# Down projection of a hybrid DiT block: three plain input tiles and twenty pairs, five pairs at a time, in place of seven plain tiles and eighteen pairs, six at a time

## The chip, the cores and the metric

The kernel runs on one core of a Trainium2 chip. The metric is the device time of one execution in microseconds (us). The kernel before was timed in three runs, and its profile is of one more execution.

## The reference

One block of a diffusion backbone over 512 latent tokens of width 2048, with 256 context tokens: a modulated norm, a combined input projection, latent attention beside a short convolution, an output projection, and a gated MLP with a depthwise convolution. All in float32. The change is in the MLP, after its up projection (5504 hidden features, 43 tiles of 128):

```python
def conv_ffn(h, w_up, cw, cb, w_down):
    u = dwconv3(h @ w_up, cw, cb)
    a, g = jnp.split(u, 2, axis=-1)
    return (a * jax.nn.silu(g)) @ w_down
...
x = x + gt_f * conv_ffn(hf_l, w_up[l], ffn_conv_w[l], ffn_conv_b[l], w_down[l])
return rms_norm(x, g_final)
```

`gt_f` is the last of six parts of a modulation vector, silu(c) times `w_ada`.

## The kernel before

Tokens lie along the free dimension (512 columns), features along the 128 partitions. A float32 operand is split into a high and a low part; a product is three matmuls (`mm3`, lines 187 to 189: high x high, high x low, low x high). ACT casts the high part of a weight, DVE subtracts it to get the low one (`split4`, lines 1023 and 1024, with three buffers each).

**Up projection** (to about 1670 us of the profile). Each hidden tile f is made by seven block products, convolved and activated (`acts`). Its result y goes one of two ways, as background work that `pump` feeds in, a piece at a time, after products. The first `STD` = 7 tiles are *plain*: `plain` (line 1050 on) writes high and low part of y to `y_d`. The other 36 make `PAIRS` = 18 pairs: `pair_sums` builds from two tiles and the two halves of the tokens seven half tiles ("11", "21", "2", "1", "3", "4", "22"), each as high and low part in one tile, and ACT sends it to `t_d`.

**Down projection, plain part.** For two halves h of the output and each plain tile k, one weight tile of 1024 columns (`dw`) is split and multiplied into eight banks of 512 columns (tiles `d`, `yl`). Between these steps the code advances `gate_mods`: 32 slices `aq` of `w_ada` (line 1301 loads, line 1303 multiplies with a vector and sums), which give the second half of the gate; they use the pool `tmp` of five buffers. It also loads the first window of pairs (`win_load`, line 1317) and, at `W0_AT`, the weights of the first block step.

**Down projection, block part.** `STEPS` = 24 steps: eight pairs of output tiles, in three rounds of six pairs of input tiles. A step does seven products of `WIN` pairs (`seven`), each of 18 matmuls of 256 columns, named p1, p2, p6, q5, p7, q4, q3 after the block scheme; q4 and q3 of a step run in the next. The names `v12p6h` and `v12p6l` are the high and low part of the weights of p6 of step 12. `into` (line 1389 for the first eight steps, 1392 later) adds a product in PSUM into the output tile `c`. `weights_of` loads four blocks of weights a step ahead and builds sums:

```python
SP.dma_start(z.a11, src[0])
SP.dma_start(z.s1, src[2])
SP.dma_start(z.a12, src[1])
V.tensor_tensor(out=z.s3, in0=z.a11, in1=z.s1, op=ALU.add)
G_.dma_start(z.s1, src[3], accum_op=ALU.add)
```

The accumulating DMA on POOL's queue (line 1345) overwrites s1, so it follows the sum s3 (line 1344); `d_p2` then adds s1 to a11 (line 1405) and a11 to a12 (line 1406) on DVE, and p6, q5 and later products use the results. `gate` (line 1456) multiplies an output tile by the gate and adds the residual `xl`, 16 times in all. Which window of pairs a step uses is given by `SLIDE`: it moves by one pair five times in a round, so that a half tile is seldom loaded twice. All half tiles of the window, the 16 outputs and the y tiles share the pool `t2` of 58 buffers; the weights share nine buffers `raw`.

**The end.** The last two steps are interleaved by hand (`za`, `zb`), with squares, the final norm (`rms_steps`), the scaling of outputs on ACT (`scale_out`, line 1470) and `final`.

The order on each engine isn't the order of the code: a scheduler simulates the program while it is built and puts each instruction where it finds it ready. An engine then runs its list in order.

Of the kernel before, what the change touches and what calls it, by code (L numbers as in the profile page):

```python
# [37 lines left out]
OUT_EARLY = 4  # L38
CTX_EARLY = 6

STD = 7
PAIRS = (NF - STD) // 2
WIN = 6

SLIDE = [0, 0, 1, 2, 3, 4, 5, 5]
STEPS = 8 * PAIRS // WIN

W0_AT = (1, 3)

AHEAD = 3  # L50

# [1 line left out]
def window(st):  # L53

    lo = SLIDE[st % 8] + st // 8 * WIN
    return [(lo + j) % PAIRS for j in range(WIN)]

# [15 lines left out]
def block_kernel(ctx, tc, xt, ctxt, ctxn, c, c_ctx, w_ada, small, w_in, w_inc, w_q, w_kv, w_out,  # L73
# [17 lines left out]
    x_d = dr.tile([NK, P, T], F32, name="x_d")  # L91
    y_d = dr.tile([STD, 2, P, T], F32, name="y_d")
    t_d = dr.tile([PAIRS, 7, P, T], F32, name="t_d")
# [45 lines left out]
    nth = {"raw": 0, "w": 0, "up": 0, "tp": 0}  # L139
# [39 lines left out]
    def part(w, i, n=1):  # L179
        return tuple(z[:, i * P:(i + n) * P] for z in w)  # L180
# [21 lines left out]
    def pump(n=1):  # L202
        while n and bg:
            if next(bg[0], bg) is bg:
                bg.popleft()
            else:
                n -= 1
# [735 lines left out]
    def two(z):  # L943
        return z[:, :T // 2], z[:, T // 2:]
# [75 lines left out]
    def split4(src, n, nm):  # L1020
        hi = rw.tile([P, 1024], F32R, tag="wh", bufs=3, name=nm + "h")
        lo = rw.tile([P, 1024], F32R, tag="wl", bufs=3, name=nm + "l")
        last_hi[:] = [A.copy(out=hi[:, :n], in_=src).ins]
        V.tensor_tensor(out=lo[:, :n], in0=src, in1=hi[:, :n].bitcast(F32), op=ALU.subtract)
        return hi, lo
# [9 lines left out]
    def acts(f, g, a):  # L1035
# [4 lines left out]
        V.tensor_tensor(out=ua, in0=ua, in1=ug, op=ALU.mult)  # L1040
        if f < STD:
            bg.append(plain(f, ua))
        elif (f - STD) % 2 == 0:
            even[0] = ua
        else:
            bg.append(pair_sums((f - STD) // 2, even[0], ua))

    even = [None]

    def plain(f, y):  # L1050

        hi, lo = hilo(y, T, f"yh{f}")
        G_.dma_start(y_d[f, 0], hi.bitcast(F32))
        yield
        G_.dma_start(y_d[f, 1], lo.bitcast(F32))
        yield
# [152 lines left out]
    def product(ps, a, n, nm, first):  # L1209

        w = split4(a, 1024, nm)
        for j in range(8):
            x = operand(n, j)
            if n in APART:
                mm2(ps, part(w, j), x, first and j == 0, j == 7, on_top=not first)
            else:
                mm3(ps[:, :256], part(w, j), x if isinstance(x, tuple) else two(x), first and j == 0, j == 7, on_top=not first)

        nth["up"] += 1
        pump(nth["up"] % 2)  # L1220

    def aside(ps, nm):
        r = cp.tile([P, 256], F32, tag="uu", bufs=4, name=nm)
# [14 lines left out]
    fetched = deque()  # L1238
    plain_order = deque((h, k) for h in range(2) for k in range(STD))

# [69 lines left out]
    gm = gate_mods()  # L1310
# [4 lines left out]
    def win_load(n, p):  # L1315
        z = win[n, p] = t2([P, T], F32R, f"w{n}_{p}")
        SP.dma_start(z.bitcast(F32), t_d[p, OPS.index(n)])

    first = [(n, p) for n in OPS for p in window(0)]
# [10 lines left out]
    def weights_of(st):  # L1330
# [4 lines left out]
        z.out, z.new = (None, None) if nxt == z.win else (z.win[0], nxt[-1])  # L1335
        n = WIN * P
        src = [w_dnw[st][:, b * n:(b + 1) * n] for b in range(4)]
# [14 lines left out]
    for h in range(2):  # L1352
        ps = [bank8(f"d{h}{i}") for i in range(8)]
        for k in range(STD):
            plain_fetch()
            if h == 0 and k + 2 < STD:
                y_load(k + 2)
            w = split4(fetched.popleft(), 1024, f"dw{h}{k}")
            for i in range(8):
                mm3(ps[i], part(w, i), y[k], k == 0, k == STD - 1)  # L1360
            pump(1)
            for _ in range(2):
                next(gm, None)
            for _ in range(2 if h == 0 else 3):
                win_load(*first.pop(0))
            if (h, k) == W0_AT:
                nxt = weights_of(0)
        for i in range(8):
            acc2.append(t2([P, T], F32, f"c{8 * h + i}"))
            A.copy(out=acc2[-1], in_=ps[i])  # L1370
    drain()

    def seven(z, ps, a, n, nm, first, pump_at=()):

        nm = f"v{z.st}{nm}"
        w = split4(a, WIN * P, nm)
        for j, p in enumerate(z.win):
            x = win[n, p]
            mm3(ps[:, :256], part(w, j), (x[:, :256], x[:, 256:]), first and j == 0, j == WIN - 1, on_top=not first)
            if j in pump_at:  # L1380
# [93 lines left out]
    for st in range(STEPS - 2):  # L1474
        z = nxt
        nxt = weights_of(st + 1)
        x_load(st + 1)
        gate(st)
        d_p1(z)
        if first:  # L1480
            for _ in range(4):
                win_load(*first.pop(0)) if first else None
        d_p2(z)
        if prev is not None:
            d_q4(prev)
        d_p6(z)
        d_q5(z)
        next(gm, None)
        if first:
            for _ in range(4):  # L1490
                win_load(*first.pop(0)) if first else None
        if prev is not None:
            d_q3(prev)
            ended(prev)
        d_p7(z)
        prev = z
# [151 lines left out]
```

## Time and profile before

| | |
|---|---|
| three runs | 2136.31, 2138.38, 2142.66 us; median 2138.38 |
| span of the profiled execution, first to last instruction | 2135.4 us |
| mean granted TensorE clock | 0.995 |
| PE, DVE, ACT busy share of the span | 98%, 85%, 49% |
| DMA, mean over the span | 241 GB/s |
| down projection: plain part | about 1670 to 1754 us |
| block part and the end | 1754 to 2135 us |

The profile's own execution is known by its span alone. PE is TensorE's matmuls, PEld its weight loads, DVE the vector engine, ACT the scalar engine, POOL and SP the engines that here mostly issue transfers. A busy PE share says that it always had a matmul under way; whether it was held up is read from the distance of the starts. A window row gives a stretch, its length, the busy time of each engine with the count of instructions, the granted clock, the mean busy share of the 16 DMA engines and GB/s. A timeline row gives start, duration, engine, line, operation, tiles (out<-in, without buffer numbers) and in brackets the idle time before it with what ended that.

### The profile page before, as it was taken

The numbers are of one execution on the slowest core, as the hardware profiler recorded it, in microseconds if no ns is written. First come the engines' busy times: TensorE is split into PE (matmuls) and PEld (weight loads), VectorE is DVE, ScalarE is ACT, GpSimd is POOL, SyncE is SP. The second block draws the span as 40 slices with busy tenths as digits, with TensorE's granted clock in tenths as the row PEclk, the third lists the DMA queues.
The fourth block names the chain that finished last, engine by engine and source line by source line (L and its number), as shares of the span: only waits on it lengthen the run. The fifth ranks groups of instructions, "written<-read, shape, count | busy, mean of one in ns | idle before, by whom it ended". The sixth has DMA issues, their size and how long they took to land.

```text
span 2135.4 us, 35321 instructions
## 1 busy us (share of the span) xinstructions
PE 2084.9 (98%) x13268; PEld 1875.9 (88%) x13268; DVE 1824.1 (85%) x3024; ACT 1047.1 (49%) x1715; POOL 117.0 (5%) x144
## 2 busy tenths in 40 slices
PE   7899999999999999999999999999999999999997
PEld 4688788888888888999999999999999889999996
DVE  7998987778896989898999999999999659888877
ACT  5533333555552337565555555555655433333445
POOL 0000000000000100011000000000000000000000
PEclk9999999999999999999999999999999999999998
DMA  9989876334459986577788788888888989878683
GB/s 335 334 281 322 286 269 202 126 117 159 168 181 355 362 287 216 138 219 210 232 236 241 223 231 243 227 234 231 237 229 232 364 300 309 254 230 240 195 260 107
DMA packets 170176, 513.75 MB, mean 241 GB/s; under 512 B 18962, under 2 KB 23314, under 8 KB 164370
## 3 DMA queue, kind: packets, MB, share of 16 engines
q1 hardware_dynamic: 133364, 418.14, 57.7%
q0 software_dynamic: 17408, 59.25, 14.1%
q10 hardware_dynamic: 19232, 34.09, 4.2%
q8 instruction: 104, 1.70, 0.3%
q14 instruction: 68, 0.56, 0.1%
HBM read 464.22 MB, written 46.14 MB: 239 GB/s over the span
## 4 chain that ended last, share of the span: by engine, by line
PE 89%; DVE 5%; DMA 4%; ACT 2%; issue 1%; SPq 0%; DVEq 0%; POOLq 0%; ACTq 0%
PE pp L187 4%; PE pp L189 4%; PE pp L188 4%; PE o L189 1%; PE o L188 1%; PE o L187 1%; PE d L187 1%; PE d L189 1%; PE d L188 1%; DMA ada<-in_w_ada 1%; PE uf L187 1%; PE uf L188 1%; PE uf L189 1%; PE of L187 1%; PE of L188 1%
## 5 line engine op out<-in xcount | busy, mean ns | idle before, releaser
L1151 POOL DMA_DIRECT2D u_s<-in_w_up x80 | 68.5, 856 | 684.1 <-DMA u_s<-in_w_up 364.4
L263 DVE SCALAR_TENSOR_TENSOR ada<-ada,sv 128x1024 f32<-128x1024 f32 x68 | 81.9, 1217 | 14.0 <-DMA ada<-in_w_ada 14.0
L166 ACT CAST w_0h<-rw 128x512 fp32r<-128x512 f32 (+1 forms) x63 | 38.3, 618 | 107.6 <-PE pp L188 62.3
L241 DVE SCALAR_TENSOR_TENSOR ada<-ada,sv 128x1024 f32<-128x1024 f32 x64 | 77.3, 1215 | 4.3 <-DMA ada<-in_w_ada 4.3
L530 DVE SCALAR_TENSOR_TENSOR ada<-ada,svc 128x1024 f32<-128x1024 f32 x64 | 75.9, 1218 | 3.0 <-DMA ada<-in_w_ada 3.0
L167 DVE TENSOR_TENSOR w_0l<-rw,w_0h 128x512 fp32r<-128x512 f32 (+1 forms) x63 | 42.5, 679 | 21.7 <-ACT w_0h L166 21.6
L263 DVE SCALAR_TENSOR_TENSOR ra<-ra,sv 128x1024 f32<-128x1024 f32 x44 | 52.4, 1215 | 1.0 <-DMA ra<-in_w_ada 1.0
L1265 DVE TENSOR_TENSOR u<-u,u_s 128x1024 f32<-128x1024 f32 x40 | 48.7, 1218 | 1.7 <-DMA u_s<-in_w_up 1.7
L1266 DVE TENSOR_TENSOR u<-u,u 128x1024 f32<-128x1024 f32 x40 | 48.6, 1215 | 0.0
L793 POOL TENSOR_TENSOR gr<-gr,half 128x8 f32<-128x8 f32 x4 | 10.1, 2522 | 631.3 <-DVE gr L792 538.9
L764 ACT CAST pth<-t 128x384 fp32r<-128x384 f32 x64 | 28.6, 485 | 26.4 <-PE t L761 26.4
L1075 DVE TENSOR_TENSOR tp<-a,tp 128x256 fp32r<-128x256 f32 x90 | 37.4, 416 | 2.6 <-ACT tp L1074 2.6
L1074 ACT CAST tp<-a 128x256 fp32r<-128x256 f32 x90 | 35.7, 403 | 4.8 <-DMA yl6h<-y_d 3.5
L1038 ACT ACTIVATE g<-g 128x512 f32<-128x512 f32 x43 | 27.3, 634 | 18.3 <-DVE g L1032 18.0
L541 DVE TENSOR_TENSOR acc<-acc,pp 128x512 f32<-128x512 f32 x50 | 33.9, 677 | 2.1 <-PE pp L189 2.1
L765 DVE TENSOR_TENSOR ptl<-t,pth 128x384 fp32r<-128x384 f32 x64 | 33.1, 547 | 2.7 <-ACT pth L764 2.7
L745 DVE TENSOR_REDUCE mn<-s 128x1 f32<-128x768 f32 x32 | 30.3, 951 | 4.6 <-PE s L734 4.6
L1030 ACT ACTIVATE g<-cg,sm 128x512 f32<-128x512 f32 x40 | 32.6, 815 | 0.0
L1030 ACT ACTIVATE a<-ca,sm 128x512 f32<-128x512 f32 x40 | 32.1, 802 | 0.0
L748 ACT ACTIVATE p<-s,mn 128x768 f32<-128x768 f32 x32 | 29.3, 915 | 1.6 <-DVE mn L745 1.3
L1031 DVE SCALAR_TENSOR_TENSOR g<-cg,sm,g 128x511 f32<-128x511 f32 x40 | 29.8, 745 | 0.0
L1031 DVE SCALAR_TENSOR_TENSOR a<-ca,sm,a 128x511 f32<-128x511 f32 x40 | 29.8, 744 | 0.0
(10238 smaller groups left out, 8906.8 us busy)
## 6 DMA issues: line engine op xcount, KB each, us to landing
ada<-in_w_ada SPq DMA_DIRECT2D x196, 512.0 KB, 6.0
u<-in_w_up SPq DMA_DIRECT2D x120, 512.0 KB, 9.0
w<-t_d SPq DMA_DIRECT2D x161, 256.0 KB, 5.3
u_s<-in_w_up SPq DMA_DIRECT2D x80, 512.0 KB, 4.0
u_s<-in_w_up POOLq DMA_DIRECT2D x80, 512.0 KB, 9.7
t_d<-tp ACTq DMA_DIRECT2D x126, 256.0 KB, 6.0
v<-in_w_dnw SPq DMA_DIRECT2D x72, 384.0 KB, 5.1
ra<-in_w_ada SPq DMA_DIRECT2D x22, 1024.0 KB, 4.7
```

The lines of the kernel that those rows point to most:

```text
L167: V.tensor_tensor(out=lo[:, :n], in0=raw[:, a:a + n], in1=hi[:, :n].bitcast(F32), op=ALU.subtract)
L187: PE.matmul(ps, w[0], x[0], start=first, stop=False, skip_group_check=on_top)
L188: PE.matmul(ps, w[0], x[1], start=False, stop=False, skip_group_check=on_top)
L189: PE.matmul(ps, w[1], x[0], start=False, stop=last, skip_group_check=on_top)
L241: V.scalar_tensor_tensor(out=r, in0=r, scalar=1.0, in1=vec[:, i * 1024:(i + 1) * 1024], op0=ALU.mult, op1=ALU.mult, accum_out=col[:, i:i + 1])
L263: keep(V.scalar_tensor_tensor(out=r, in0=r, scalar=1.0, in1=svs[i], op0=ALU.mult, op1=ALU.mult, accum_out=lc[:, t % 4:t % 4 + 1] if i else ...
L530: keep(V.scalar_tensor_tensor(out=raw[q], in0=raw[q], scalar=1.0, in1=svc[:, q * 1024:(q + 1) * 1024], op0=ALU.mult, op1=ALU.mult, accum_o ...
L1030: A.activation(u, src, AF.Identity, bias=s("fb", m), scale=s("fw", 86 + m))
L1031: V.scalar_tensor_tensor(out=u[:, 1:], in0=src[:, :T - 1], scalar=s("fw", m), in1=u[:, 1:], op0=ALU.mult, op1=ALU.add)
L1151: G_.dma_start(r[-1], src[more], accum_op=ALU.add)
L1265: V.tensor_tensor(out=a11, in0=a11, in1=s1, op=ALU.add)
L1266: V.tensor_tensor(out=a12, in0=a12, in1=a11, op=ALU.add)
```

## The change

Four plain tiles become two more pairs, and the block part takes five pairs at a time in four rounds: 32 steps of 7 x 15 matmuls, where 24 steps of 7 x 18 stood. The plain part shrinks from 14 steps to 6. So do the places at which the slices `aq` and the first window are issued in the code; both are taken in larger portions, and up to two slices in each of the first seven block steps. In the up projection `pump` runs after each of the first twelve products, and after every second one from then on. `W0_AT` moves to the second half's second tile.

```diff
-STD = 7
+STD = 3
 PAIRS = (NF - STD) // 2
-WIN = 6
-SLIDE = [0, 0, 1, 2, 3, 4, 5, 5]
+WIN = 5
+SLIDE = [0, 0, 1, 2, 2, 3, 4, 4]
 STEPS = 8 * PAIRS // WIN
-W0_AT = (1, 3)
+W0_AT = (1, 1)
...
         nth["up"] += 1
-        pump(nth["up"] % 2)
+        pump(1 if nth["up"] <= 12 else nth["up"] % 2)
...
             pump(1)
-            for _ in range(2):
+            for _ in range(3):
                 next(gm, None)
-            for _ in range(2 if h == 0 else 3):
-                win_load(*first.pop(0))
+            for _ in range(5 if h == 0 else 6):
+                if first:
+                    win_load(*first.pop(0))
...
         d_p6(z)
         d_q5(z)
-        next(gm, None)
+        if st < 7:
+            for _ in range(2):
+                next(gm, None)
```

Counted in the built programs: loads of window half tiles 161 before, 168 now; loads of block weights (SP) 96 and 128; accumulating loads (POOL) 24 and 32; plain weights 14 and 6. Line numbers behind the plain loop grow by one: `into` is 1390 and 1393, the first weight sum 1406, `gate` 1457, `scale_out` 1471.

**DVE ahead of the first block product.** `v0p1l` is the low part of its weights, `dw` those of the plain part, `ts`, `a` and `tp` belong to the last pair's half tiles. Before:

```order
2267 L1024 TENSOR_TENSOR dw13l<-d_17796,dw13h 128x1024
2268 L1024 TENSOR_TENSOR dw14l<-d_17843,dw14h 128x1024
2269 L1303 SCALAR_TENSOR_TENSOR aq_17722,lcc<-aq_17722,svq_17417 128x512
2270 L1303 SCALAR_TENSOR_TENSOR aq_17763,lcc<-aq_17763,svq_17417 128x512
2271 L1024 TENSOR_TENSOR dw15l<-d_17885,dw15h 128x1024
2272 L1303 SCALAR_TENSOR_TENSOR aq_17766,lcc<-aq_17766,svq_17419 128x512
2273 L1303 SCALAR_TENSOR_TENSOR aq_17832,lcc<-aq_17832,svq_17419 128x512
2274 L1303 SCALAR_TENSOR_TENSOR aq_17835,lcc<-aq_17835,svq_17417 128x512
2275 L1024 TENSOR_TENSOR dw16l<-d_17927,dw16h 128x1024
2276 L1024 TENSOR_TENSOR v0p1l<-v_17969,v0p1h 128x768
```

Now:

```order
2269 L1303 SCALAR_TENSOR_TENSOR aq_17581,lcc<-aq_17581,svq_17461 128x512
2270 L1075 TENSOR_TENSOR tp_17624<-ts_17569,tp_17624 128x256
2271 L1303 SCALAR_TENSOR_TENSOR aq_17629,lcc<-aq_17629,svq_17461 128x512
2272 L1303 SCALAR_TENSOR_TENSOR aq_17632,lcc<-aq_17632,svq_17459 128x512
2273 L1075 TENSOR_TENSOR tp_17700<-a_17303,tp_17700 128x256
2274 L1075 TENSOR_TENSOR tp_17753<-a_17449,tp_17753 128x256
2275 L1303 SCALAR_TENSOR_TENSOR aq_17635,lcc<-aq_17635,svq_17459 128x512
2276 L1075 TENSOR_TENSOR tp_17818<-ts_17569,tp_17818 128x256
2277 L1303 SCALAR_TENSOR_TENSOR aq_17705,lcc<-aq_17705,svq_17461 128x512
2278 L1024 TENSOR_TENSOR v0p1l<-v_17778,v0p1h 128x640
```

The last pair's half tiles and six slices now stand right ahead of that split. In all, 17 slices stood ahead of it and 11 stand there now; in SP's queue the load of the eleventh is behind 20 of the 35 window tiles.

**DVE in the third block step (step 2).** `v2p1l`, `v2p2l` and `v2p6l` are its first splits, `c<-c,v2a` an addition of its first product, line 1456 or 1457 a gating. Before:

```order
2324 L1024 TENSOR_TENSOR v2p2l<-v_18266,v2p2h 128x768
2325 L1456 SCALAR_TENSOR_TENSOR c_17772<-c_17772,mod,xl_19418 128x512
2326 L1307 TENSOR_TENSOR mod<-mod,sm 128x8
2327 L1405 TENSOR_TENSOR v_18264<-v_18264,v2s_18265 128x768
2328 L1389 TENSOR_TENSOR c_17778<-c_17778,v1a 128x256
2329 L1024 TENSOR_TENSOR v1q4l<-v_18120,v1q4h 128x768
2330 L1308 TENSOR_SCALAR gn<-mod 128x16
2331 L1389 TENSOR_TENSOR c_17780<-c_17780,v2a 128x256
2332 L1406 TENSOR_TENSOR v_18266<-v_18266,v_18264 128x768
2333 L1024 TENSOR_TENSOR v2p6l<-v_18264,v2p6h 128x768
```

Now:

```order
2323 L1303 SCALAR_TENSOR_TENSOR aq_18119,lcc<-aq_18119,svq_17459 128x512
2324 L1390 TENSOR_TENSOR c_17655<-c_17655,v2a 128x256
2325 L1024 TENSOR_TENSOR v2p2l<-v_17996,v2p2h 128x640
2326 L1024 TENSOR_TENSOR v1q4l<-v_17872,v1q4h 128x640
2327 L1303 SCALAR_TENSOR_TENSOR aq_18122,lcc<-aq_18122,svq_17461 128x512
2328 L1390 TENSOR_TENSOR c_17655<-c_17655,v2b 128x256
2329 L1303 SCALAR_TENSOR_TENSOR aq_18293,lcc<-aq_18293,svq_17461 128x512
2330 L1390 TENSOR_TENSOR c_17653<-c_17653,v1a 128x256
2331 L1406 TENSOR_TENSOR v_17994<-v_17994,v2s_17995 128x640
2332 L1407 TENSOR_TENSOR v_17996<-v_17996,v_17994 128x640
2333 L1303 SCALAR_TENSOR_TENSOR aq_18296,lcc<-aq_18296,svq_17459 128x512
2334 L1024 TENSOR_TENSOR v2p6l<-v_17994,v2p6h 128x640
```

No slice was left in this step before; now there are seven. The addition of the first product stands ahead of the second split, and the weight sum behind the addition of the second product.

**ACT near the end.** `out<-c` is a scaling, the casts are the high parts of weights; `v21q3h` and `v23p6h` before answer to `v29q3h` and `v31p6h` now. Before:

```order
1751 L1470 ACTIVATE out_22603<-c_17786,sm 128x256
1752 L1023 CAST v21q3h<-v_21910 128x768
1753 L1470 ACTIVATE out_22606<-c_18100,sm 128x256
1754 L1470 ACTIVATE out_22606<-c_18102,sm 128x256
1755 L1470 ACTIVATE out_22609<-c_18104,sm 128x256
1756 L1470 ACTIVATE out_22609<-c_18106,sm 128x256
1757 L1470 ACTIVATE out_22708<-c_17772,sm 128x256
1758 L1470 ACTIVATE out_22708<-c_17774,sm 128x256
```

Now:

```order
1811 L1023 CAST v29p7h<-v29s_22549 128x640
1812 L1471 ACTIVATE out_23159<-c_17655,sm 128x256
1813 L1471 ACTIVATE out_23159<-c_17657,sm 128x256
1814 L1023 CAST v30p1h<-v_22718 128x640
1815 L1471 ACTIVATE out_23162<-c_17659,sm 128x256
1816 L1471 ACTIVATE out_23162<-c_17661,sm 128x256
1817 L1023 CAST v30p2h<-v_22720 128x640
1818 L1471 ACTIVATE out_23165<-c_17843,sm 128x256
```

Eleven scalings moved ahead, between casts of earlier products; a block of twelve remains behind `v30p6h`.

## The prediction

> **What bounds the kernel now.** I read the page's busy times first, then the windows of 15 us over the down projection, then the timeline of single engines there. The page names TensorE (PE):
>
> ```profile
> PE 2084.9 (98%) x13268; PEld 1875.9 (88%) x13268; DVE 1824.1 (85%) x3024; ACT 1047.1 (49%) x1715; POOL 117.0 (5%) x144
> ```
>
> The windows (columns: stretch, length, busy us of PE, PEld, DVE, ACT, POOL, granted clock, DMA share, GB/s) split the down projection in three. In the first rows, the plain tiles, PE is full, DVE half idle and the DMA engines full. From 1758 on, the block products, PE is full and DVE at 97 to 98% for two windows, later at 12.3 of 15. Near the end PE has holes and ACT is full.
>
> ```profile
> 1698.00:1713.00 15.00, 15.00 (x66) 12.08 (x65) 7.03 (x13) 5.27 (x9) 0.00 (x0) 1.00 1.05 391
> ...
> 1758.00:1773.00 15.00, 15.00 (x129) 15.00 (x128) 14.50 (x30) 5.86 (x7) 0.00 (x0) 1.00 1.00 371
> 1773.00:1788.00 15.00, 15.00 (x129) 15.00 (x128) 14.68 (x28) 5.86 (x7) 1.42 (x2) 1.00 0.89 277
> ...
> 1953.00:1968.00 15.00, 15.00 (x128) 15.00 (x128) 12.34 (x17) 5.85 (x7) 0.85 (x1) 1.00 0.74 221
> ...
> 2088.00:2103.00 15.00, 12.85 (x95) 12.44 (x94) 10.55 (x15) 13.94 (x30) 0.00 (x0) 0.90 0.27 75
> ```
>
> So PE work saved counts in full, unless DVE, the queue of transfers or ACT takes the place of PE. The granted clock is 1.00 in all but the last of these rows, so I price PE at one rate.
>
> **PE work, term one.** Rows of the chain and of PE's timeline:
>
> ```profile
> 1703.93 1.87 PE d L187 x8
> 1884.83 0.28 PE L187 MATMUL v9a<-w,v9p1h 128*128 128x256 f32 x1
> 2004.44 0.28 PE L187 MATMUL v17a<-w,v17p1h 128*128 128x256 f32 x1
> ```
>
> Eight matmuls of 512 columns take 1.87 us, 0.2338 each. From the first matmul of step 9 to that of step 17 lie eight steps of 126 matmuls of 256 columns: 119.61 us, 14.95 a step, 0.1187 each. Removed: 4 plain tiles x 16 output tiles x 3 matmuls = 192 of 512 columns, 44.9 us. Added: 32 steps x 105 less 24 x 126 = 336 of 256 columns, 39.9 us. Net -5.0 us. A step becomes 12.46 us. Both prices stand in the trace in the same stages, so this term has no range.
>
> **DVE in the first block steps, term two.** Each step has ten wide DVE operations (seven splits, three weight sums), now 640 columns and not 768, and seven additions of a product into the output. DVE starts the next instruction before the last one's length is over, so I take start to start:
>
> ```profile
> 1931.15 0.95 DVE L1024 TENSOR_TENSOR v11q4l<-v,v11q4h 128x768 fp32r<-128x768 f32 x1
> 1932.02 0.48 DVE L1392 SCALAR_TENSOR_TENSOR c<-v12a,mod,c 128x256 f32<-128x256 f32 x1
> ...
> 2050.28 0.69 DVE L355 TENSOR_TENSOR ssq<-ssq,eq 128x512 f32<-128x512 f32 x1
> 2050.88 0.48 DVE L1392 SCALAR_TENSOR_TENSOR c<-v19a,gn,c 128x256 f32<-128x256 f32 x1
> 2051.27 0.95 DVE L1406 TENSOR_TENSOR v<-v,v 128x768 f32<-128x768 f32 x1
> ...
> 1755.93 0.68 DVE L1303 SCALAR_TENSOR_TENSOR aq<-aq,svq 128x512 f32<-128x512 f32 x1
> 1756.54 0.08 DVE L1303 DVE_READ_ACCUMULATOR aq<-aq,svq 128x1 f32 x1
> 1756.54 0.42 DVE L1389 TENSOR_TENSOR c<-c,v0a 128x256 f32<-128x256 f32 x1
> 1756.87 0.68 DVE L1303 SCALAR_TENSOR_TENSOR aq<-aq,svq 128x512 f32<-128x512 f32 x1
> ...
> 1775.18 0.74 DVE L1456 SCALAR_TENSOR_TENSOR c<-c,mod,xl 128x512 f32<-128x512 f32 x1
> 1775.84 0.95 DVE L1024 TENSOR_TENSOR v1p7l<-v1s,v1p7h 128x768 fp32r<-128x768 f32 x1
> ```
>
> 768 columns take 0.87, 512 take 0.60, so 640 some 0.74 by the line between them (0.60 and 0.87 are its ends); an addition 0.33 in the first eight steps, 0.39 later; a slice of the gate's dot product (aq) 0.61; a gating of an old output (line 1456) 0.66. Bare steps then need 10 x 0.74 + 7 x 0.33 = 9.7, later 10.1 of 12.46 us, which leaves room. But the order puts 21 of the 32 slices behind the first block product, where 15 stood, since six plain steps drain fewer of them than fourteen. Counting DVE's rows from the first split of a step to that of the next, with these prices: step 0, 9.7 us; step 1 (six slices, a gating) 14.0; step 2 (seven, two) 15.3; step 3 (four, two) 13.7. That is 52.7 us against PE's 26 products x 15 x 0.1187 = 46.3, 6.4 us too much. The same count for before gives 14.0, 14.8, 12.6 and 12.3 against 14.95, and PE stayed dense in it. From step 4 on it is 11.1 and less.
>
> A lead would hide this: with three buffers for the low halves DVE could be three products, 5.3 us, ahead of PE. It isn't at the start, because eleven slices stand ahead of the first split, and the eleventh comes late in the queue of transfers. Rows of SP's and PE's timeline and of the DMA view for 1668 to 1743:
>
> ```profile
> 1663.47 0.38 SPq L1325 DMA_DIRECT2D yl0h<-y_d  x1
> 1754.17 0.28 PE L187 MATMUL v0a<-w,v0p1h 128*128 128x256 f32 x1
> DMA packets 13894, 28.75 MB, mean 383 GB/s; under 512 B 1545, under 2 KB 1545, under 8 KB 13889
> aq<-in_w_ada SPq DMA_DIRECT2D x22, 256.0 KB, 6.3
> ```
>
> From the first y tile to that slice the queues carry 6 y, 20 window tiles, 11 slices, 6 stores and two residual tiles of 0.262 MB, 2 plain weights and 2 halves of the vector of 0.524 MB, and 9 weight blocks of 0.328 MB: 16.8 MB, 44 us at 383 GB/s, so 1707 if the queue starts at 1663 as before. The plain tiles end at 1754.2 - 44.9 = 1709.3. The slice and the split take 1.3 us: a tie, and no lead. I add 1 us for the tie (0 to 3) and 1 for additions that wait in DVE's fixed order for a product that itself waits for DVE (step 2 has an addition ahead of the split it holds up). Term two: +8 (1 if a lead of 5.3 us is built up after all, 12 if the wide operations cost nearer 0.87). The DMA is no third bound there: a slice more or less only shifts it by 0.7 us.
>
> [...]
>
> **The accumulated weight sum, term three.** Each step builds a sum in DVE (line 1344), sends an accumulating DMA from POOL behind it, and DVE then waits for it at line 1405 in its fixed order, with the second split of the step queued behind.
>
> ```profile
> 1948.75 0.96 DVE L1344 TENSOR_TENSOR v14s<-v,v14s 128x768 f32<-128x768 f32 x1
> 1957.25 0.96 DVE L1405 TENSOR_TENSOR v<-v,v14s 128x768 f32<-128x768 f32 x1
> ...
> 2056.13 0.95 DVE L1344 TENSOR_TENSOR v21s<-v,v21s 128x768 f32<-128x768 f32 x1
> 2064.08 0.96 DVE L1405 TENSOR_TENSOR v<-v,v21s 128x768 f32<-128x768 f32 x1 [2.17 <-DMA v21s<-in_w_dnw]
> 2072.07 0.95 DVE L1344 TENSOR_TENSOR v22s<-v,v22s 128x768 f32<-128x768 f32 x1
> 2081.11 0.96 DVE L1405 TENSOR_TENSOR v<-v,v22s 128x768 f32<-128x768 f32 x1 [3.24 <-DMA v22s<-in_w_dnw]
> L189 PE MATMUL v22b<-w,v22p2l 128*128 128x256 f32 x6 | 1.8, 299 | 0.6 <-DVE v22p2l L1024 0.6
> ```
>
> In the middle the way takes 8.5 us with no wait. Where the DMA decided, it took 8.0 and 9.0; a DVE wait of 2.2 cost PE nothing at that split, 3.2 cost 0.6. Steps shorter by a sixth shorten the 8.5 to 7.1, and an addition that the new order moves ahead of the sum takes 0.4 more: 6.7. With 320 KB and not 384 the DMA needs some 7 to 7.7 (an estimate: the sum's own 0.13 and up to a sixth of the transfer). So DVE will wait 0.3 to 1 us in most steps; its spare 2.3 us a step pays for that, and PE bears about 1.9. Six steps (5, 6, 10 and 28 to 30) have the sum one split later, as steps 20 to 22 had, and come near that. I take +1.5 (0 to 4).
>
> **The end, term four.** Before, ACT makes 19 scalings of outputs in a row, one cast among them, and PE waits for the cast behind them:
>
> ```profile
> 2093.83 4.50 ACT L1470 ACTIVATE out<-c,sm 128x256 f32<-128x256 f32 x11
> 2098.24 0.81 ACT L1023 CAST v23p6h<-v 128x768 fp32r<-128x768 f32 x1
> L187 PE MATMUL v23a<-w,v23p6h 128*128 128x256 f32 x6 | 2.5, 411 | 1.7 <-ACT v23p6h L1023 1.7
> ```
>
> Fewer window tiles leave buffers free, so the new order puts 11 scalings between earlier casts, where ACT is half idle, and 12 in a block. A scaling takes 4.50 / 11 = 0.41 us, so ACT has about seven, 2.9 us, less ahead of that cast. But PE has two shorter products less to do meanwhile, 2 x 3 x 0.1187 = 0.7. From the wait of 1.7 at most that can be won: -1 (-3, with the small waits around it, to +2, if the block of 12 holds up another cast).
>
> **Edits at nothing.** The up projection makes 20 x 7 half tiles and three plain tiles in place of 18 x 7 and seven; its later pairs already run so, with PE dense and DVE at 92%, by this window:
>
> ```profile
> 1151.90:1448.50 296.60, 296.60 (x2042) 275.83 (x2041) 271.50 (x399) 172.88 (x262) 25.58 (x30) 1.00 0.83 233
> ```
>
> The extra pumping touches its first two steps, where only the plain tiles' stores are waiting. If that cover fails, a pair costs DVE 11 x 0.33 against two plain tiles' 2 x 0.60, 2.4 us more, twice. Seven more window tiles (1.8 MB) and 32 weight sums for 24 go through queues that were 0.74 busy in the middle. The last additions, the final norm and the stores don't change.
>
> **The sum.** -5.0 + 8 + 1.5 - 1 = +3.5 us. The profiled execution spans 2135.4 us, 3.0 below the median of the runs, 2138.38; what makes up the 3.0 the trace doesn't show, and I carry it. 2138.9 + 3.0 = 2142.
>
> **Rivals.**
> *DVE keeps its lead.* If the eleven slices land earlier (the queue idles less, or their transfers overtake others), DVE enters step 0 some 5 us ahead, term two falls to 1 to 2, and PE's saving shows: -5.0 + 1.5 + 1.5 - 1 = -3, at best -8 with terms three and four at their low ends: 2130 to 2136. For it: DVE at 97% in 1758 to 1788 cost PE nothing. Against: that was below a full step, 15.3 in 12.5 isn't.
> *The accumulated sum decides every step (slower).* Place: line 1405, the second split behind it. It decides from about 6.7 + 1.9 = 8.6 us between the sum's start and the landing; above shows 8.0 and 9.0 with 384 KB. If it takes 9.1, each of some 22 steps loses 0.5: +11, so 2142 - 1.5 + 11 = 2151 or more. Against: 320 KB, and windows at 0.74 DMA share in the middle.
> *The queue at the start is later (slower).* Slices need a free temporary buffer before SP issues them and hold up the window tiles behind them; should the eleventh land 5 us after my 1707, term two grows by 5: 2147.
>
> **How the numbers follow.** Forecast 0.5 (2135 to 2147), DVE's lead 0.25 (2130 to 2136), the sum 0.1 (2151 and above), the queue 0.15 (2145 to 2150). About 0.3%, 6.4 us, is what a measurement of this kernel can tell from no change: below 2132.0 is faster, above 2144.8 slower. Faster: half of the second case, 0.12, and 0.05 of the first, should terms two and four both fall low: 0.17. Slower: the last two cases, 0.25, and 0.1 of the first: 0.35. Same: 0.48. The range 2131 to 2151 takes in the bounds of terms two to four and leaves out the third case but for its start, and some tails.
>
> **What would show it.** Right: the plain stage ends 45 us sooner; a step in the middle (10 to 25) takes 12.46 us with PE dense; in steps 1 to 3 DVE is full and PE has holes of 5 to 9 us in all, released by DVE's splits; DVE waits at the weight sum (now line 1406) in most steps without a hole in PE; the wait of PE for the cast in the end is shorter. Wrong: no holes in PE in steps 0 to 4 (term two), steps of over 12.6 us in the middle (term three), or more than 10 us of holes behind step 28 (term four).

## The result and the profile after

The changed kernel takes 2169.95 us (median of four runs, 2168.64 to 2173.24), the kernel before 2137.51 in runs beside it: ratio 1.0151, 95% interval 1.0137 to 1.0165. It is slower by 32 us, and outside the predicted range. The profiled execution took 2169.14 us, with a span of 2167.4, which is 32.0 more than the span of before. Of all runs used below one, of the kernel without slices (e5), was in a slow state, 2271.68 us at a granted clock of 0.849, and is left out.

The page of after, its busy times, then the windows by stage (columns as in the prediction; the stages are plain part, steps 0 to 3, 4 to 11, 12 to 27, 28 to the last product):

```profile
PE 2093.3 (97%) x13412; PEld 1886.3 (87%) x13412; DVE 1865.8 (86%) x3170; ACT 1061.5 (49%) x1773; POOL 119.5 (6%) x144
```

```profile
1680.40:1729.70 49.30, 40.77 (x176) 33.09 (x177) 25.90 (x51) 15.99 (x28) 1.71 (x2) 0.93 0.95 320
1729.70:1783.80 54.10, 48.86 (x378) 46.80 (x377) 52.49 (x114) 21.30 (x35) 2.56 (x3) 0.97 1.03 364
1783.80:1891.60 107.80, 103.28 (x856) 101.78 (x855) 89.62 (x150) 41.40 (x57) 6.83 (x8) 1.00 0.80 237
1891.60:2091.50 199.90, 199.90 (x1682) 199.65 (x1681) 171.38 (x276) 84.75 (x118) 13.69 (x16) 1.00 0.76 223
2091.50:2154.40 62.90, 57.46 (x466) 55.45 (x464) 51.53 (x88) 40.17 (x77) 2.56 (x3) 1.00 0.42 112
```

PE is dense only in the fourth row. Before, it was dense from the plain part to step 11. What PE's bare work takes and what lies over it follow. From v0p1 on, the bare work is at the prices of the prediction; for the up projection it is the length of before, for the plain part that length less the 44.9 us:

| stage, from first matmul to first matmul | before | after | bare work after | over it |
|---|---|---|---|---|
| up projection, u6p1 to u8p1 | 39.6 | 49.8 | 39.6 | 10.2 |
| plain part, dw00 to v0p1 | 84.1 | 49.3 | 39.2 | 10.1 |
| steps 0 to 3, v0p1 to v4p1 | 55.9 | 54.1 | 46.3 | 7.8 |
| steps 4 to 11, v4p1 to v12p1 | 119.6 | 107.8 | 99.7 | 8.1 |
| from v12p1 to the last product | 192.8 | 262.8 | 252.8 | 10.0 |

Before has 0.3 over its bare work in steps 0 to 3 and 9.1 in the last row. So 46.2 less 9.4 less the 5.0 us of PE work saved is 31.8, and the spans differ by 32.0. There are four new losses of 8 to 10 us each. They arise as follows.

**The up projection.** The timeline of ACT in after. A pair's operand is cast (line 1074) and sent off (line 1076):

```profile
947.70 1.01 ACTq L1076 DMA_DIRECT2D t_d<-tp  x2
...
950.17 0.33 ACTq L1076 DMA_DIRECT2D t_d<-tp  x1
...
961.81 0.40 ACT L1074 CAST tp<-a 128x256 fp32r<-128x256 f32 x1 [8.40 <-DMA t_d<-tp]
...
963.54 1.03 ACT L1023 CAST u7p2h<-u 128x1024 fp32r<-128x1024 f32 x1
```

Three stores leave within 3 us, and the next operand needs the buffer of one of the first two. Its cast waits 8.4 us for that store and starts some 13 to 14 us after the store's issue (the trace has no landing for it). In ACT's fixed order the cast of u7p2's weights stands behind it. PE's timeline:

```profile
960.22 0.29 PE L189 MATMUL u7a<-hf14h,u7p1l 128*128 128x256 f32 x1
964.62 0.80 PE L196 MATMUL u7b<-hf,u7p2h 128*128 128x512 f32 x1 [4.11 <-ACT u7p2h L1023]
```

Before sends the same three stores, but over 5.4 us, and the next cast comes 3.9 us behind the third of them; the first two had landed in 5.8 us, and nothing waits:

```profile
1022.17 0.82 ACTq L1076 DMA_DIRECT2D t_d<-tp  x2
...
1027.52 0.33 ACTq L1076 DMA_DIRECT2D t_d<-tp  x1
...
1031.46 0.40 ACT L1074 CAST tp<-a 128x256 fp32r<-128x256 f32 x1
```

**The plain part.** PE, ACT and DVE around the change from the first half to the second:

```profile
1711.55 0.79 PE L187 MATMUL d<-yl0h,dw10h 128*128 128x512 f32 x1 [8.53 <-ACT c L1371]
...
1707.74 0.41 ACT L1074 CAST tp<-ts 128x256 fp32r<-128x256 f32 x1 [3.87 <-DVE ts L1080]
1710.52 0.35 ACTq L1076 DMA_DIRECT2D t_d<-tp  x1
1710.91 4.01 ACT L1371 COPY c<-d 128x512 f32<-128x512 f32 x8 [2.77 <-DVE tp L1075]
...
1699.13 0.69 DVE L1303 SCALAR_TENSOR_TENSOR aq<-aq,svq 128x512 f32<-128x512 f32 x1 [0.27 <-DMA svq<-sv_d]
...
1709.45 0.69 DVE L1303 SCALAR_TENSOR_TENSOR aq<-aq,svq 128x512 f32<-128x512 f32 x1 [0.46 <-DMA aq<-in_w_ada]
...
1710.07 0.42 DVE L1075 TENSOR_TENSOR tp<-ts,tp 128x256 fp32r<-128x256 f32 x1
...
1723.70 0.69 DVE L1303 SCALAR_TENSOR_TENSOR aq<-aq,svq 128x512 f32<-128x512 f32 x1 [0.47 <-DMA aq<-in_w_ada]
```

Read it from the end: PE waits for a bank, whose copy (line 1371) stands in ACT's order behind an operand of the last pair; ACT issues that store only when DVE has the low half; DVE has gate slices ahead of it, which wait for their loads. In the view of the chain that ended last, two of these loads stand ahead of the put:

```profile
1699.86 5.30 DMA aq<-in_w_ada
...
1705.97 3.46 DMA aq<-in_w_ada
```

The rows of 1699.13 and 1723.70 are the first and the last of the eleven slices ahead of the first block product. The prediction had the eleventh at 1707, from 16.8 MB at 383 GB/s. The DMA view for 1665 to 1724:

```profile
DMA packets 9111, 18.65 MB, mean 316 GB/s; under 512 B 1012, under 2 KB 1012, under 8 KB 9107
```

**Steps 0 to 11.** In step 2 PE waits for a cast of p6's weights, ACT for the sum, and in step 9 DVE waits for the accumulating DMA:

```profile
1761.04 0.72 ACT L1023 CAST v2p6h<-v 128x640 fp32r<-128x640 f32 x1 [6.16 <-DVE v L1406]
1761.82 0.39 PE L187 MATMUL v2a<-w,v2p6h 128*128 128x256 f32 x1 [2.08 <-ACT v2p6h L1023]
...
1759.78 0.42 DVE L1390 TENSOR_TENSOR c<-c,v1a 128x256 f32<-128x256 f32 x1 [0.51 <-PE v1a L189]
1760.12 0.82 DVE L1406 TENSOR_TENSOR v<-v,v2s 128x640 f32<-128x640 f32 x1
...
1851.76 0.83 DVE L1406 TENSOR_TENSOR v<-v,v9s 128x640 f32<-128x640 f32 x1 [2.28 <-DMA v9s<-in_w_dnw]
1852.50 0.75 DVE L1457 SCALAR_TENSOR_TENSOR c<-c,mod,xl 128x512 f32<-128x512 f32 x1
1853.16 0.82 DVE L1024 TENSOR_TENSOR v9p2l<-v,v9p2h 128x640 fp32r<-128x640 f32 x1
1854.03 0.39 PE L189 MATMUL v9b<-w,v9p2l 128*128 128x256 f32 x1 [1.22 <-DVE v9p2l L1024]
```

In step 2 the sum itself stands in DVE's order behind additions of products, and DVE waited 0.56 and 0.51 us for PE at two of them, while PE was about to wait for the sum. In step 9, a wait of 2.3 us at the weight sum, and a gating of 0.66 that the order puts between the sum and the split, make 1.2 us in PE.

### The profile page after: what moved, and what is told of

Its sections match the earlier page's. It is cut to its first block, busy times and chain, and to the rows that moved or that the text cites. A ratio compares the mean times of both kernels' runs of the same rounds, so it can differ in the third digit from the quotient of the medians.

```text
span 2167.4 us, 35997 instructions
## 1 busy us (share of the span) xinstructions
PE 2093.3 (97%) x13412; PEld 1886.3 (87%) x13412; DVE 1865.8 (86%) x3170; ACT 1061.5 (49%) x1773; POOL 119.5 (6%) x144
## 3 DMA queue, kind: packets, MB, share of 16 engines
q0 software_dynamic: 17920, 58.20, 13.8%
## 4 chain that ended last, share of the span: by engine, by line
PE 82%; DVE 7%; DMA 6%; issue 2%; ACT 2%; SPq 0%; DVEq 0%; ACTq 0%; POOLq 0%
PE pp L187 4%; PE pp L189 4%; PE pp L188 4%; PE o L188 1%; PE o L189 1%; PE o L187 1%; PE uf L187 1%; PE uf L188 1%; PE of L187 1%; PE of L188 1%; PE uf L189 1%; PE of L189 1%; PE pf L188 1%; PE pf L189 1%; PE pf L187 1%
## 5 line engine op out<-in xcount | busy, mean ns | idle before, releaser
L167 DVE TENSOR_TENSOR w_0l<-rw,w_0h 128x512 fp32r<-128x512 f32 (+1 forms) x63 | 42.7, 684 | 21.2 <-ACT w_0h L166 21.1
L1075 DVE TENSOR_TENSOR tp<-a,tp 128x256 fp32r<-128x256 f32 x100 | 41.8, 419 | 9.2 <-ACT tp L1074 9.2
L1074 ACT CAST tp<-a 128x256 fp32r<-128x256 f32 x100 | 39.7, 404 | 12.9 <-DMA t_d<-tp 8.4
L793 POOL TENSOR_TENSOR gr<-gr,half 128x8 f32<-128x8 f32 x4 | 10.1, 2522 | 628.6 <-DVE gr L792 536.2
L1303 DVE SCALAR_TENSOR_TENSOR aq<-aq,svq 128x512 f32<-128x512 f32 x32 | 21.9, 687 | 11.3 <-DMA aq<-in_w_ada 10.9
```

The source lines that it names most:

```text
L167: V.tensor_tensor(out=lo[:, :n], in0=raw[:, a:a + n], in1=hi[:, :n].bitcast(F32), op=ALU.subtract)
L1075: V.tensor_tensor(out=z[:, 256:], in0=src, in1=z[:, :256].bitcast(F32), op=ALU.subtract)
```

## The experiments

Totals are a poor measure of one place: the part ahead of u3p1, which no edit touches, took 880.1 to 887.8 us in the fourteen profiles. So each stage is judged by its own length in the profiled execution (us, first matmul to first matmul); medians are of the timed runs.

| kernel | median | u7 to u8 | plain | steps 0-3 | 4-11 | 12-27 | 28 to last product |
|---|---|---|---|---|---|---|---|
| bare work | | 19.8 | 39.2 | 46.3 | 99.7 | 199.4 | 53.4 |
| after | 2169.95 | 29.6 | 49.3 | 54.1 | 107.8 | 199.9 | 62.9 |
| e1 late puts | 2166.48 | 19.8 | 51.5 | 54.0 | 109.6 | 201.8 | 62.7 |
| e2 copies first | 2178.21 | 28.1 | 51.6 | 56.4 | 108.8 | 203.2 | 62.8 |
| e3 slices loaded only | 2173.68 | 28.9 | 50.7 | 51.6 | 106.5 | 204.7 | 63.0 |
| e4 sum on DVE | 2159.22 | 28.1 | 51.3 | 57.8 | 100.5 | 201.8 | 57.5 |
| e5 no slices | 2153.55 | 28.3 | 39.2 | 46.8 | 106.3 | 205.0 | 62.7 |
| e6 slices later | 2186.67 | 28.2 | 42.4 | 54.4 | 121.6 | 210.5 | 63.1 |
| e7 gatings later | 2175.64 | 28.9 | 48.0 | 53.6 | 108.4 | 210.4 | 62.6 |
| e8 combined | 2145.39 | 19.8 | 43.4 | 49.0 | 104.3 | 203.8 | 57.5 |
| e9 combined, second | 2152.36 | 19.8 | 39.2 | 53.6 | 113.1 | 202.4 | 60.0 |
| e10 slices even | 2159.85 | 19.8 | 42.7 | 53.2 | 113.5 | 202.9 | 60.0 |
| e11 combined, third | 2142.68 | 19.8 | 39.2 | 50.1 | 105.8 | 205.4 | 57.5 |
| e12 sum mixed | 2156.51 | 19.8 | 39.8 | 53.2 | 107.2 | 211.0 | 57.8 |

Theory A: four separate waits. Its rivals name one shared, overfull resource (the queues, or DVE). The forecasts of totals were poor: of theory A's twelve only e11's came true, and e5's was missed by 1.5 us; of the rivals' twelve only e12's. What follows rests on the stages.

**e1, the first pair's last operands put later.**

```diff
-        pump(1 if nth["up"] <= 12 else nth["up"] % 2)
+        pump(0 if nth["up"] in (27, 29) else 1 if nth["up"] <= 12 or nth["up"] in (100, 200) else nth["up"] % 2)
```

> Edit: the first pair's last two operands are put one product pair later (no pump at products 27 and 29, one each at 100 and 200). Theory A: ACT's cast of the operand behind the one ring buffer whose store takes 12.9 us holds up the cast of u7p2h that stands behind it in ACT's order; the 4.1 us hole and the short waits and slow matmuls behind it go. u7 to u8 falls from 29.6 to about 20 us, total -10: 2159 to 2161 us. Rival: the weights of u7 come late because the queues are overfull, and the put is only hit by the same delay: the hole stays, total -3 at most, 2167 or more.

The timeline of ACT in e1: u7p2h is cast at once, the operand 10 us later without a wait.

```profile
958.47 1.04 ACT L1023 CAST u7p2h<-u 128x1024 fp32r<-128x1024 f32 x1
...
968.16 0.40 ACT L1074 CAST tp<-a 128x256 fp32r<-128x256 f32 x1
```

u7 to u8 falls from 29.6 to 19.8 us: theory A holds for this place, with its price. A store of the burst still took 13.0 us to land there; now nothing stands behind it. The median fell by 3.5 only, and the profiled execution was no shorter than that of after: it began 4 us later, the plain part, steps 4 to 11 and steps 12 to 27 were each some 2 us longer, and the extra put at product 200 made a hole of 1.3.

**e2, the bank copies ahead of the put.**

```diff
-            pump(1)
+            pump(0 if (h, k) == (0, 2) else 2 if (h, k) == (1, 0) else 1)
```

> Edit: no operand of the last pair is put behind the third plain tile of the first half, two behind the next one. Theory A: the eight copies of the banks stand in ACT's order behind that put, which waits for DVE, which stands behind gate slices that wait for their loads; the 8.9 us hole before dw10 goes and the plain stage ends about 10 us sooner. Some slices and the put move behind the first block product, so steps 0 to 3 grow by 3 to 6 of it: total -4 to -8, 2162 to 2166 us. Rival: the hole is a wait for transfers (the queue is full there), the copies only stand beside it: the hole stays over 6 us, total 2168 to 2172.

The hole before dw10 is gone, yet the plain part is 2.3 us longer. The waits of PE in e2 from 1690 on, and ACT's timeline:

```profile
PE v0a L187 <- ACT c L1371: 12.2, 1, 12.2
```

```profile
1723.54 0.40 ACT L1074 CAST tp<-ts 128x256 fp32r<-128x256 f32 x1 [3.83 <-DMA w<-t_d]
1728.99 0.33 ACTq L1076 DMA_DIRECT2D t_d<-tp  x1
1729.36 4.01 ACT L1371 COPY c<-d 128x512 f32<-128x512 f32 x8 [5.42 <-DMA w<-t_d]
```

The second set of copies now stands behind a put, and with it v0p1. The put's low half was ready at 1727.5, behind slices whose loads DVE had waited for; for the last 1.5 us up to the store, the profile names the load of a window tile. Theory A had the order of ACT right and the gain wrong: the slices were still there. Its total (2162 to 2166) and the rival's (2168 to 2172) were both passed, at 2178.21.

**e3, slices loaded but not used, and e5, no slices.** In e3:

```diff
+                if 4 * i + q < 19:
                     V.scalar_tensor_tensor(out=r, in0=r, scalar=1.0, in1=svq[q], ...)
```

> This kernel leaves out the dot products of the last 13 of the 32 gate slices (their loads stay), so its gates are not the reference's. Theory A: in block steps 0 to 3 DVE has more work than PE; without 13 x 0.61 us the 54.1 us from the first to the fifth step's first matmul become 46.3 to 48, total -6 to -8: 2162 to 2164 us. Rival: the transfers, at a DMA share of 0.98 to 1.06 there, set the pace: 53 to 54 us stay, total 2169 to 2170.

e5 drops the load and the product of all 32.

> This kernel leaves out all 32 gate slices, their loads and their dot products, so its gates are not the reference's; it is a bound, not a version. Theory A: the plain stage's hole is a chain that begins at the slices' loads (DVE waits for them, ACT's put for DVE, the bank copies for the put, PE for the copies): the plain stage, 49.3 us from dw00 to v0p1, falls to 39 to 41, and steps 0 to 3 from 54.1 to 47 to 50. Total -12 to -15 us, 2155 to 2158. Rival: the window tiles' own transfers hold the first product (35 tiles and the weights, some 20 MB from the first y tile on): the hole moves to v0p1, the stage stays over 46 us, total 2163 or more.

The windows of e5, plain part and steps 0 to 3, and the waits of ACT in e3 between 1750 and 1766:

```profile
1677.90:1717.10 39.20, 39.20 (x177) 32.14 (x178) 20.29 (x31) 17.22 (x30) 1.70 (x2) 1.00 1.02 346
1717.10:1763.80 46.70, 46.50 (x391) 46.32 (x390) 39.30 (x66) 21.49 (x33) 2.55 (x3) 1.00 0.95 304
```

```profile
ACT v2p6h L1023 <- DVE v L1408: 5.7, 1, 5.7
ACT v2p2h L1023 <- DMA v<-in_w_dnw: 3.3, 1, 3.3
```

Without slices PE is dense in both stages: the 10.1 us of the plain part and 7.4 of the 7.8 in steps 0 to 3 come with them. The window tiles, 35 of them, are in time. Of the 7.4, the products of the 13 late slices make 2.6 (e3: 51.6 for 54.1); the other 4.8 come with the loads and the eight earlier products behind v0p1, which no run separates. In e3 a load of step 2's own weights comes late (3.3 us), which fits a part of the loads. So e3 decides against both pure readings, 46.3 to 48 and 53 to 54. Its total, 2173.68, is above both forecasts: steps 12 to 27 were 4.8 us longer and the profile began 4 us later.

**e4, the weight sum on DVE.**

```diff
-        G_.dma_start(z.s1, src[3], accum_op=ALU.add)
         SP.dma_start(z.a22, src[3])
+        V.tensor_tensor(out=z.s1, in0=z.s1, in1=z.a22, op=ALU.add)
```

> Edit: the accumulating DMA of each step's weight sum is replaced by an addition on DVE of the block that is loaded anyway. Theory A: in steps 4 to 11 PE's holes come from the way of the sum through the DMA (6.5 to 8.6 us from sum to landing, DVE waits 0.6 to 2.8 us); 107.8 us from v4p1 to v12p1 become 100 to 102, total -5 to -8: 2162 to 2165 us; steps 12 to 25 stay at 12.46 although DVE has 0.74 us more in each. Rival: DVE's total load (11.2 of 13 us) decides: with 0.74 more in each step 107.8 stays or grows, total 2170 to 2176.

The windows of e4 for steps 0 to 3 and 4 to 11:

```profile
1726.40:1784.20 57.80, 51.36 (x392) 48.66 (x391) 56.65 (x120) 21.75 (x35) 0.00 (x0) 0.97 0.93 337
1784.20:1884.60 100.40, 100.40 (x842) 100.25 (x841) 93.71 (x156) 40.88 (x56) 0.00 (x0) 1.00 0.70 221
```

Steps 4 to 11 are dense although DVE does 4 us more there: the sum's way through the DMA made the holes. Behind step 28 it won 5.4 us as well, which no theory had: in after, DVE waited 2.2 to 2.6 us there at the sums of steps 28 to 30, and PE behind it. In steps 0 to 3, where DVE is full, the stage is 3.7 us longer.

**e6, slices later, and e7, gatings later.** Both queue loads on SP behind the weights of a step (`sp_last`, the load of a22):

```diff
+                with tc.issue_after(sp_last[0]) if sp_last else ExitStack():
+                    SP.dma_start(r, w_ada[88 + i][:, q * T:(q + 1) * T])
...
-            for _ in range(3):
+            for _ in range(2):
                 next(gm, None)
...
-        if st < 7:
+        if st < 10:
```

> Edit: two slices for each plain tile in place of three, the rest two in each of the steps 0 to 9, each load queued behind its step's weights. Theory A: fewer slices stand ahead of the first product (7 for 11): dw00 to v0p1 falls from 49.3 to 41 to 45, steps 0 to 3 from 54.1 to 50 to 53, steps 4 to 11 grow by 0 to 3 as DVE gets the slices there: total -5 to -10, 2160 to 2165. Rival: slices only change places, DVE's work in steps 0 to 11 is what it was: what is won in the plain stage is given back, 2168 to 2172.

```diff
+                with tc.issue_after(sp_last[0]):
+                    SP.dma_start(xl[m], x_d[m])
```

> Edit: the loads of the residual tiles are queued behind the weights of their own step, so that the 16 gatings of old outputs stand in steps 7 to 14 and not in 1 to 9. Theory A (DVE's work and late weights share the excess in steps 0 to 3): five or six gatings of 0.66 us and their loads less there: 54.1 us to 50 to 52, total -2 to -4, 2166 to 2168. Rival (the weights of step 2 alone, which come late behind window tiles and slices in SP's queue): 53 to 55 stay, total 2169 to 2171.

The waits of DVE, in e6 over steps 4 to 11, in e7 over 12 to 27:

```profile
DVE aq L1304 <- DMA aq<-in_w_ada: 13.3, 8, 5.3
DVE v L1410 <- DMA v9s<-in_w_dnw: 3.9, 1, 3.9
```

```profile
DVE c L1459 <- DMA xl<-x_d: 6.6, 4, 3.1
DVE v L1407 <- DMA v20s<-in_w_dnw: 3.2, 1, 3.2
```

e6 wins 6.9 us in the plain part and gives 13.8 back in steps 4 to 11, where DVE, in order, waits for late slices and late sums, and 10.6 more in steps 12 to 27. e7 wins 0.5 in steps 0 to 3 and loses 10.5 in 12 to 27. So theory A failed in both. The rivals had the direction, that nothing is won, but not the loss: they allowed 2172 and 2171 us at most. That what is moved there meets the sums of the accumulating DMA is how I read these waits; it is not shown by them alone.

**e8, combined** (e1, e4, e6 and e7 together).

> Edits together: the first pair's puts later, the weight sum on DVE, slices and gatings later. Theory A, four costs that add up: the up projection -10, the plain stage -5 to -8, steps 0 to 3 -2 to -4 (the sum on DVE costs there some 3), steps 4 to 11 -7, the end -5: 2136 to 2143 us, about the kernel before. Rival, one overfull resource (DVE, now 0.74 us more a step) behind all of them: the holes move on, 2150 or more.

2145.39 us, ratio to before 1.0034 (1.0019 to 1.0049): 24.6 of the 32 us are back, 2 us short of theory A's range, and the median is well below the rival's 2150. The stages do not simply add up: against after, the up projection, the plain part, steps 0 to 3 and the end give 9.8, 5.9, 5.1 and 5.4 us, as forecast or a little more, but steps 4 to 11 give 3.5 and not 7, and steps 12 to 27 lose 3.9. The edits of e6 and e7, which lose by themselves, win here: against e4, the plain part and steps 0 to 3 are 7.9 and 8.8 us shorter, steps 4 to 27 are 5.8 longer.

**e9 and e10, the plain part's order.** To e8, e9 adds: no slice behind the first two plain tiles and three behind each other; two or three slices in each of the first eight steps; the sum on DVE queued behind the split of p2; the extra puts at 58 and 100. e10 is e9 with two slices behind each plain tile. The edit of e9, against after:

```diff
+        with tc.issue_after(last_lo[0]):
+            V.tensor_tensor(out=z.s1, in0=z.s1, in1=z.a22, op=ALU.add)
...
-            for _ in range(3):
+            for _ in range(0 if h == 0 and k < 2 else 3):
                 next(gm, None)
...
-        if st < 7:
-            for _ in range(2):
+        if st < 8:
+            for _ in range(3 if st in (3, 4, 5, 6) else 2):
```

> As the combined kernel, and: no slice behind the first two plain tiles and three behind each of the others, so that the last pair's puts find DVE free and the bank copies stand ahead of the next put; the sum on DVE queued behind the second split, where the block that it adds has landed; the two extra puts at products 58 and 100. Theory A: the hole of 2.7 us before dw10 goes, the waits of DVE for a22 (0.4 to 2.2 us) and their holes of about 1 us in steps 7 to 14 go, 1.5 us in the up projection go: 2145.4 less 6 to 9, 2136 to 2139 us. Rival: DVE is at its limit in steps 1 to 8 (some 12 of 12.46 us), the gain is lost there: 2142 to 2147.

> As the kernel before in this call, but two slices behind each of the six plain tiles, as in the combined kernel: in ACT's order a put that waits for DVE stands ahead of the bank copies again. Theory A: the hole before dw10 comes back at 2 to 3 us: 2 to 3 us slower than that kernel, 2138 to 2142. Rival (the put costs nothing as long as few slices stand ahead): the same within 1 us.

The plain part does what theory A said: 39.2 with the put behind the copies, 42.7 with slices and put ahead of them. The forecasts of the totals fell, 2152.36 and 2159.85 us for at most 2147 and 2142. The waits of DVE in e9:

```profile
DVE aq L1304 <- DMA aq<-in_w_ada: 11.9, 11, 2.4
```

Three sums in a row now stand between p2 and the cast of p6, and slices wait for loads: 113 us for 104 in e8. The late place of the sum was a mistake of mine; which part of the 9 us it makes and which the slices make was not separated.

**e11 and e12.** e11 is e8 with e9's plain part and puts, the sum early, and slices 1 a step in steps 0 to 2, then 2. e12 has the sum on DVE only in steps 4 to 11 and 28 to 31.

```diff
+        own_sum = 4 <= st < 12 or st >= 28
+        if not own_sum:
+            G_.dma_start(z.s1, src[3], accum_op=ALU.add)
         sp_last[:] = [SP.dma_start(z.a22, src[3]).ins]
+        if own_sum:
+            V.tensor_tensor(out=z.s1, in0=z.s1, in1=z.a22, op=ALU.add)
```

> As the first combined kernel (sum on DVE early, in the order of that kernel), with no slice behind the first two plain tiles, three behind each other one, one in each of the steps 0 to 2 and two in each later one, and the extra puts at products 58 and 100. Theory A: the plain stage stays at 39.2 us (43.3 in the first combined kernel), the up projection gains 1.5, steps 0 to 3 stay at 49 to 51, steps 4 to 11 at 104 to 106: 2145.4 less 2 to 6, 2139 to 2143 us. Rival: each slice taken from the plain stage costs its 0.61 us and its late load in the steps: 2145 to 2150.

> As the kernel before in this call, with the weight sum on DVE only in steps 4 to 11 and 28 to 31, by the accumulating DMA elsewhere. Theory A (the sum's way hurts only where DVE or the queues are late anyway): steps 0 to 3 1 to 3 us shorter, steps 12 to 27 at 200 and not 204: 3 to 6 us faster than that kernel, 2134 to 2139. Rival (the accumulating DMA's way of 6 to 9 us hurts wherever it stands): 2 us slower or more.

e11 is the best of the new versions, 2142.68 us, within what was expected, and still slower than the kernel before: 1.0024 (1.0011 to 1.0037). From v0p1 on it lies 20.0 us over its bare work, where before has 9.4; the 5.0 us that the change saves do not make up for that. In e12 the rival held: 211.0 us in steps 12 to 27 for 205.4, with DVE waiting at the sums up to 3.6 us.

## Why the prediction was wrong

**The step that failed first is "edits at nothing".** It let the up projection pass with the words that its later pairs "already run so, with PE dense". The later pairs do; the first pair does not. Its puts come in a burst, and it now starts during f = 5, straight behind the plain tiles' stores, in a ring of three buffers. That cost 10.2 us, and e1 brings 9.8 of it back. The price of 2.4 us that I set in case the cover fails was for DVE's work; what failed was a buffer, and ACT's order behind it. The changed line of `pump` that I looked at leaves ACT's order of instructions around u7 as it is without it; no run takes it out alone. Where the trace has their landing, stores of line 1076 took up to 12.9 us in the up projection of after (the third of the burst), and at most 10.3 in before; why, the traces do not tell.

**The start of the block part.** The prediction called it a tie, plus 0 to 3 us, and gave 0.15 to a later queue with a price of 5. The place was right, the price 10.1. Two numbers failed: 18.65 MB went through, not 16.8, and at 316 GB/s, not 383: SP, which issues the loads, waited 5.3 us in these 59 at slices whose buffer DVE had not freed, and more behind other work. And the way to PE was another than the split of v0p1 that I looked at: put, then bank copies, on ACT. e5, e2 and e9 show it. Before has such a put too, but with seven tiles a half it is over in time, and the copies wait only for PE, as ACT's timeline shows:

```profile
1705.52 0.33 ACTq L1076 DMA_DIRECT2D t_d<-tp  x1
...
1711.90 3.52 ACT L1370 COPY c<-d 128x512 f32<-128x512 f32 x7 [1.51 <-PE d L189]
```

**Term two** foresaw 8 us in steps 0 to 3 and 7.8 came, in the steps that it named, and with additions that wait for PE ahead of a sum that PE needs. But the longest hole, 2.1 us, ended with a cast on ACT and not with a split on DVE. Leaving out the 13 last products, 7.9 us of the work that I counted, won only 2.6. Leaving the DMA out of it ("a slice more or less only shifts it by 0.7 us") had no ground: with the loads gone too, 7.4 us went. So the size was right partly by chance.

**Term three** was +1.5 (0 to 4); steps 4 to 11 lost 8.1, and e4 gives 7.3 of it back. The mechanism was the one described, the size was not. From the view of the line of the accumulating DMA in after (who waited for it, us, times; and its time to landing):

```profile
  DVE v L1406: 35.5, 26
DMA to landing us min/median/max: 4.8/5.7/8.4
```

That is 1.4 us in each of 26 steps, where I had 0.3 to 1. And PE's tolerance of 1.9 was taken from a split that follows the sum at once; in steps 7 to 9 a gating stands between them. The rival for it (2151, from a loss in every one of some 22 steps) did not come: steps 12 to 27 were dense in this profile.

**Term four** was -1; the stretch from v12p1 on is 0.9 worse than before. The wait for the cast, 1.7 us before, is gone; waits at the sums of steps 28 to 30 ate that up, as e4 shows with its 5.4 us.

**Term one** holds: steps 12 to 27 take 12.50 us each, for 12.46, and e5's plain part is 39.2, exactly 44.9 less than before.

In sum, -5.0 + 8 + 1.5 - 1 became -5.0 + 7.5 + 8.1 + 0.9 + 10.2 + 10.1. What stays open: why the sums in steps 12 to 27 are in time in after and late in e7 and e12. Each wait there is seen, its cause in the queues is not.

## What to carry to other kernels

A change that shortens a stage also shortens the time in which its side work was hidden: count that side work (loads, stores, copies of banks) against the new length, not only the engine that you save on. Where an engine runs its list in order, look for the instruction that waits for a buffer or a DMA and ask what stands behind it; the price is that of the wait, not of the instruction (in u7 a cast of 0.40 us waited 8.4 us). When one of several waits is removed, measure the stage and not the total, since the next wait takes over, as in e2, e6 and e7.

## What the runs showed of the hardware

A short hole in PE cost more than its length in e12: 2.2 us, and 1.6 us more in the matmuls behind it. The windows of e12 around a hole of 2.2 us in step 16 (from start to start), then those of e6 around one of 2.56 in step 13, the third number from the end being the granted clock:

```profile
1930.60:1934.00 3.40, 1.50 (x13) 1.29 (x12) 1.86 (x3) 0.85 (x2) 0.00 (x0) 0.99 0.54 190
1934.00:1937.40 3.40, 3.40 (x18) 3.40 (x18) 3.31 (x7) 0.72 (x1) 0.00 (x0) 0.50 0.17 38
...
1915.20:1918.60 3.40, 1.86 (x16) 1.66 (x14) 0.88 (x2) 0.73 (x1) 0.00 (x0) 1.00 0.99 311
1918.60:1922.00 3.40, 2.66 (x21) 2.64 (x22) 3.40 (x6) 1.45 (x2) 0.00 (x0) 1.00 0.32 77
```

Behind the hole of e12, seventeen matmuls of 256 columns came 0.21 us apart in place of 0.119, 1.6 us in all. Behind the longer hole of e6 the clock stayed at 1.00, so length alone does not decide. In after the clock was at half three times from u3 to the last product, behind the holes of 4.11, 8.53 and 2.08 us. The windows of after ahead of each such stretch and over it, then two around the hole of 1.22 us in step 9:

```profile
960.16:963.58 3.42, 0.35 (x3) 0.13 (x2) 1.04 (x2) 1.77 (x4) 0.00 (x0) 1.00 0.29 114
963.58:973.82 10.24, 7.71 (x21) 5.85 (x22) 10.24 (x16) 5.58 (x10) 0.00 (x0) 0.50 0.33 99
...
1704.27:1707.68 3.41, 0.00 (x0) 0.00 (x0) 3.29 (x8) 0.00 (x0) 0.00 (x0) 1.00 0.65 233
1707.68:1714.51 6.83, 2.96 (x7) 2.38 (x8) 2.35 (x8) 4.00 (x9) 0.86 (x1) 0.50 0.84 224
...
1758.88:1762.30 3.42, 1.34 (x10) 0.95 (x8) 2.88 (x6) 1.26 (x2) 0.00 (x0) 1.00 1.05 392
1762.30:1765.71 3.41, 3.28 (x15) 3.14 (x15) 3.41 (x7) 0.72 (x2) 0.00 (x0) 0.50 1.05 389
...
1851.04:1854.45 3.41, 2.19 (x18) 1.98 (x18) 2.69 (x5) 1.12 (x2) 0.00 (x0) 1.00 0.72 240
1854.45:1857.87 3.42, 3.42 (x31) 3.42 (x30) 3.42 (x6) 1.06 (x2) 0.00 (x0) 1.00 0.49 173
```

The three stretches last 10.24, 6.83 and 3.41 us, three, two and one times 3.413. They start 744.10 and 54.62 us apart, 218 and 16 times that, and 3.1, 4.7 and 2.6 us after their holes began. In the 3.41 us ahead of them PE was busy for 0.35, 0.00 and 1.34 us. With 2.19 us busy, in step 9, full clock followed. The stretch at half in before, 3.41 us from 2100.09 on, stands behind 1.26 us busy; in the windows of e12 and e6 above it is 1.50 us, then half clock, and 1.86 and 2.66 us at full clock. What sets the clock is not shown by these few cases. Behind the long holes of after, matmuls of 512 columns came 0.43 apart for 0.234; in the up projection that makes some 4 of the 10 us, by an estimate from the second row: PE was busy for 7.71 us at half the clock.
